# Two more seven-product pairs in a layer's first FFN, with their sums in the mixer and the ahead-splits gathered at one pair

## The chip, the cores and the metric

The kernel runs on one core of a Trainium2 chip. The metric is the device time of one execution in microseconds (us). Engines are named as in the profile: PE (matrix products; PEld is its loading of weights), DVE (vector), ACT (scalar), POOL (GpSimd) and SP, which here only issues DMA transfers. Each engine runs its instructions strictly in the order in which they were built; an instruction whose input, buffer or transfer is not ready holds up all behind it on its engine.

## The reference: what is computed

Two layers of a decoder trunk on 512 tokens plus 16 learned ones (528 columns), model width 1024. Each layer is a mixer (attention, two kinds of convolution, an output projection) and a gated FFN with 2816 hidden columns and a short causal convolution. The change touches the FFN of the first layer and what is prepared for it. Cut down:

```python
def ffn_sublayer(h, pre_g, post_g, w_up, conv_w, w_down):
    u = rms_norm(h, pre_g)
    z = jnp.einsum("bld,df->blf", u, w_up)
    z = causal_depthwise_conv(z, conv_w)
    g, up = jnp.split(z, 2, axis=-1)
    y = jnp.einsum("blf,fd->bld", jax.nn.silu(g) * up, w_down)
    return h + rms_norm(y, post_g)

for l in range(DEPTH):
    h = mixer_sublayer(h, ...)
    h = ffn_sublayer(h, ...)
```

## The kernel before

**Exact products in three passes.** Every float32 operand of a large product is split into a high part (a cast on ACT, `whi`, `shi`, `uhi`) and a low part (a subtraction on DVE, `wlo`, `slo`, `ulo`). A product is high by high, high by low, low by high. The 528 columns go in two halves of 264.

**The FFN.** The 2816 hidden columns are 22 blocks of 128. A *pair* f is block f of the gate and block f of the up-projection. Pairs run in three parts of 8, 7 and 7 (`PARTS`); after each part comes a stage *down*, eight output blocks m, whose results ACT copies (`yp`, L2410) or DVE adds. An ordinary pair is 2 blocks x 8 chunks of the width x 3 passes x 2 halves = 96 matmuls (L837).

**Seven products.** Some pairs are computed after Strassen's manner: the pair is a 2 x 2 block product, done as seven products of blocks (L2288) and not eight, 84 matmuls. For that the weights must be there as sums of blocks, which are made ahead into a DRAM tile `w_sum`, and taken from it as the blocks "c", "b" and "d". Weight block "b" is split into the tiles `shi` and `slo`, of which there is one buffer each; "c" goes to `whi`, `wlo` (three buffers). In a seven-product pair ACT copies the finished banks of PSUM to `zs` (L2373), which frees a bank for a later product of the same or the next pair.

**Who makes the sums.** `SUMS` has, for each layer, five places: ahead of time in the layer before; in the mixer; by *ticks* in the FFN (each pair, one step); in *down* of part 0; in *down* of part 1. In the mixer and by ticks a pair's sum is three copies from DRAM to DRAM, issued by SP (L545: two of 256 KB, one of 512 KB), and then three adding transfers issued by POOL (L534: 512 KB, 256 KB, 256 KB), each of which waits until the one before has landed. In *down* it is two loads by POOL into a spare tile, four additions on DVE and two stores by POOL (L589 to L601).

**The mixer's planner.** In the mixer a planner in the program (`Flow`) keeps a clock of its own for every engine and writes all engines' orders by costs and due times. The copies of the i-th pair in the mixer are due `SUM_EVERY * i` = 40 us of its clock apart, with priority 8; each transfer is planned at 0.9 us and 9 us until it has landed:

```python
for i, f in enumerate(sums_at(l, 1)):
    copies, *adds = sum_steps(l, f)
    tok = flow.op("sp", 2.0, copies, (Tok(flow.pe + SUM_EVERY * i),), prio=8, lat=SUM_LAT)
    for op in adds:
        tok = gp(SUM_US, op, tok, prio=8, lat=SUM_LAT)
```

On POOL the mixer also runs the causal masks of attention (L1651, tiles `p` and `pf`, exponentials that ACT makes at L1644). PE reads a masked tile in the product with the values (L1671).

**Ahead-splits.** While the FFN of layer 0 runs, six chunks of layer 1's input projection are loaded, split and stored to DRAM (`store_one`, L661 to L675): SP loads a chunk (L675), in a later call ACT casts it to `shi` (L666) and DVE subtracts to `slo` (L667), and POOL stores both (L670). They use the same single buffers `shi` and `slo` as block "b". `AHEAD_SPLITS` says at which pair f of the program the seven calls are written (f = 8 is the first pair of part 1); where their instructions stand on the engines is then set by the program's scheduler.

**h.** After part 0's pairs the tile `h` is copied to DRAM (L2384 and L2385, two transfers by SP) and is used as a spare buffer for weights from then on; it is loaded back after the last seven-product pair.

Of the kernel before, what the change touches and what calls it, by code (L numbers as in the profile page):

```python
# [18 lines left out]
KD = D // P  # L19
# [9 lines left out]
PARTS = (8, 7, 7)  # L29


SUMS = (((), (11, 12, 13), (15, 16), (17, 18), (19, 20)),
        ((8, 9), (10, 11, 12, 13), (15, 16), (17, 18), (19, 20)))
SEVEN = tuple(sorted(sum(places, ())) for places in SUMS)
NEXT_SUMS, AHEAD_SPLITS = 13, (8, 8, 9, 9, 10, 10, 11)
SUM_US, SUM_LAT, SUM_EVERY = 0.9, 9.0, 40.0
K2 = KD // 2
SB = K2 * P
# [351 lines left out]
def tile_hybrid_trunk(ctx: ExitStack, tc: tile.TileContext, xT, wflat, pv_d, out):  # L390
    nc = tc.nc
# [3 lines left out]
    def T(pool, shape, dt, tag, bufs=None):  # L395
        uid[0] += 1
        kw = {} if bufs is None else {"bufs": bufs}
        return pool.tile(list(shape), dt, tag=tag, name=f"{tag}_{uid[0]}", **kw)
# [92 lines left out]
    def load_h(pool, src, prio=0):  # L491

        t = T(pool, [P, KD, L], F32, "h", 1)
        at = {(hf, k0): flow.op("sp", dma_us(2 * H), lambda k0=k0, hf=hf: nc.sync.dma_start(
            t[:, k0:k0 + 2, half_sl(hf)], src[:, k0:k0 + 2, half_sl(hf)]), prio=prio + 3 * hf, lat=dma_lat(2 * H))
            for hf in range(2) for k0 in range(0, KD, 2)}
        return t, at

    dram = ctx.enter_context(tc.tile_pool(name="dram", bufs=1, space=bass.MemoryType.DRAM))
    h_dram = T(dram, [P, KD, L], F32, "h_dram")  # L500
# [48 lines left out]
    def sums_at(l, place):  # L549

        return SUMS[l][place] if l < DEPTH else ()

# [132 lines left out]
    def next_w():  # L685
        prefetch(1 + AHEAD)
        return ready.popleft()[1]
# [158 lines left out]
    def two(t):  # L846
        return t.rearrange("p (a b) -> p a b", a=2)
# [1181 lines left out]
    with tc.tile_pool(name="pre", bufs=2, reuse_waits="tile") as sp, tc.manual_schedule(engines=every):  # L2029
# [7 lines left out]
        h, h_at = load_h(sp, xT)  # L2037
# [56 lines left out]
    for l in range(DEPTH):  # L2094
# [23 lines left out]
        with tc.tile_pool(name=f"fp{l}", bufs=2, reuse_waits="tile") as fp:  # L2118
# [35 lines left out]
            with tc.manual_schedule(engines=every):  # L2154
                flow.yields = YF
                h, h_at = load_h(fp, xT if l == 0 else h_dram)
# [40 lines left out]
            seven = SEVEN[l]  # L2197
# [141 lines left out]
            def finish_pair():  # L2339
                if late_ups:  # L2340
                    late_ups.popleft()()
# [3 lines left out]
            for part, nf in enumerate(PARTS):  # L2345
                for f in range(f0, f0 + nf):
                    if g:
                        tick(g[max(g)][0][:, :1])
                    for _ in range(AHEAD_SPLITS.count(f) if l == 0 else 0):
                        store_one()  # L2350
                    if f in seven:
                        seven_pair(f)
                        if f == seven[-1]:
                            spare[0] = None
                            with tc.issue_after(last_load[0].ins):
                                for k in range(0, KD, 2):
                                    nc.sync.dma_start(h[:, k:k + 2], h_dram[:, k:k + 2])
                        continue
                    finish_pair()
                    if seven and f == 2:  # L2360
                        building[0] = normalised()
                    for i in (2 * f, 2 * f + 1):
                        if i < len(zs):
                            continue
                        if i < FIRST["w_out"]:
                            scaled(i, [first.ps[hf, i] for hf in range(2)])
                            continue
                        w = next_w()
                        ps = mmt((6, 2)[i % 2]) if ts else mmt()
                        mm3({hf: ps[:, hf, :iws[hf]] for hf in range(2)}, w, range(KD), u_in)  # L2370
                        if ts:
                            for (a, z), hf in zip(i_spans, range(2)):
                                nc.scalar.copy(zs[i % len(zs)][:, off + a - i0:off + z - i0], ps[:, hf, :z - a])  # L2373
                            continue
                        scaled(i, [ps[:, :, :H]] if i0 == 0 else [ps[:, hf, :iws[hf]] for hf in range(2)])
                    g[f] = ffn_gate(f)
                    if building[0] is not None and f < PARTS[0] - 1:
                        with tc.issue_after(mul_ins[0].ins):
                            build(5)
                finish_pair()  # L2380
                ks = list(range(nf))
                grhs = lambda b, k, hf, f0=f0: g[f0 + k][b][:, fw * hf:fw * (hf + 1)]
                if seven and part == 0:
                    for k in range(0, KD, 4):  # L2384
                        nc.sync.dma_start(h_dram[:, k:k + 4], h[:, k:k + 4])  # L2385
                    spare[0] = h
                if part < len(PARTS) - 1:
                    more = down_sums(l, part)
                    for op in more.pop(-1):
                        op()  # L2390
                    for some in ((0, 1), *((m,) for m in range(2, KD))):
                        ws = [next_w() for _ in some]
                        tiles = [mmt((4, 6, 2)[m % 3]) if seven else mmt() for m in some]
                        for group in (ks[:-1], ks[-1:]):
                            for w, ps in zip(ws, tiles):
                                where = {"start": group[0] == ks[0], "stop": group[-1] == ks[-1]}
                                if final:
                                    mm3({0: ps[:, 0, :2 * fw]}, w, group, lambda b, k, hf, f0=f0: g[f0 + k][b][:, :2 * fw], **where)
                                else:
                                    mm3({hf: ps[:, hf, :fw] for hf in range(2)}, w, group, grhs, **where)  # L2400
                        if building[0] is not None:
                            with tc.issue_after(glo_ins[0].ins):
                                build(99)
                        for m, ps in zip(some, tiles):
                            if final:
                                d, src = yp[:, m, t0:], ps[:, 0, :2 * fw]
                            else:
                                d, src = two(yp[:, m, t0:]), ps[:, :, :fw]
                            if part == 0:
                                evac = glo_ins[0] = nc.scalar.copy(d, src)  # L2410
                            else:
                                evac = nc.vector.tensor_add(d, d, src)
                            for op in more.pop(m, ()):
                                with tc.issue_after(evac.ins), tc.issue_after(last_low[0].ins):
                                    op()
                else:
                    assert not todo and not later and building[0] is None
                    if seven:
                        pools.pop().close()
                        pools.append(ExitStack())  # L2420
                        wx[0] = pools[1].enter_context(tc.tile_pool(name=f"wz{l}", bufs=WIDE, side="right", reuse_waits="tile"))
                    gpre = None if final else pvs[l + 1][1][:, _COLS["mix_pre_g"]:]
                    first = raw = rzs = None
                    if not final:
                        raw = list(zip(*[g[f0 + k] for k in range(nf)], y_pair(nf)))
                        raw = [[[t[:, half_sl(hf)] for t in ts] for ts in raw] if hf < 2 else None for hf in range(2)]
                        rzs = [rz[:, half_sl(hf)] if raw[hf] else None for hf in range(2)]
                        first = First(lambda b, k, hf, raw=raw: raw[hf][b][k] if raw[hf] else u_rhs(b, k, hf), [H, H], {})
                    with tc.issue_after(ghi_ins[NF - 2].ins), tc.manual_schedule(engines=every):
                        plan_begins()  # L2430
                        norms.factors([rs, zs[0][:, 2:]], h=APART)
                        flow.yields = YE
                        if not final:
                            plan_w(after_down, WE)
                        plan_w(len(chunks) if final else after_mixer[l + 1])
                        t_last = {nf - 2: [Tok(flow.now + 3.5)], nf - 1: [Tok(flow.now + 7.5)]}
                        finish(norms, h, {}, o_spans, ks, grhs, lambda k: t_last.get(k, []), yp,
                               gains("ffn_post_g"), gpre, SPLIT["ffn_w_down"], first, raw=raw, rzs=rzs, u_at=u_at)
                f0 += nf
# [51 lines left out]
```

## Time and profile before

| | us |
|---|---|
| profiled execution | 1262.1 |
| its span in the trace | 1260.4 |
| runs | 1263.05, 1264.51, 2452.8 |
| median of the three | 1264.51 |

One of the three runs took 2452.8 us, so that the median is the higher of the other two; the profiled execution lies within 0.2% of both. The page gives busy times of each engine, the chain of waits that ended last, groups of instructions by line, and the DMA issues with their median time to landing. The views of windows give busy time in chosen stretches, those of the timeline single instructions: start, duration, engine, line, operation, tiles, and in brackets the idle time before it on its engine with what ended it. Tiles' buffer numbers are left out.

### The profile page before, as it was taken

The page shows a single profiled execution, that of the slowest core. Times are in us where ns is not written, and L with a number is a line of the kernel's source. Part 1 is how long each engine was busy: PE and PEld are TensorE (multiplying, and loading weights), DVE is VectorE, ACT ScalarE, POOL GpSimd, SP SyncE. Part 2 cuts the span into 40 slices and gives each one's busy share as a digit, 9 for nine tenths or more (in the row PEclk, how much of TensorE's full clock was granted, in tenths as well). Part 3 has the DMA queues.
Part 4 walks back from the last instruction along what each step waited for, and adds up shares of the span by engine and source line. Part 5 has one row for each costly group of instructions (what it writes and reads, how often), then busy time and mean ns, then how long its engine had stood idle before and what let it go on. Part 6 is the DMA issues. An engine that isn't in the chain of part 4 may idle for free.

```text
span 1260.4 us, 24292 instructions
## 1 busy us (share of the span) xinstructions
PE 1244.2 (99%) x9554; PEld 1194.4 (95%) x9554; DVE 926.0 (73%) x1581; ACT 710.3 (56%) x1377; POOL 175.9 (14%) x360
## 2 busy tenths in 40 slices
PE   8999999999999999999999999999999999999997
PEld 8999898999999999999999988999999899989997
DVE  7887866589874776487688877756799748757954
ACT  7254576655444663476673545775554447526763
POOL 1323411001111001010003244110022000000000
PEclk9999999999999999999999999999999999999999
DMA  7267551726658755765652684547166565465611
GB/s 245 80 154 180 122 118 47 256 88 150 185 146 339 243 192 153 243 193 169 209 186 68 157 194 109 144 116 238 70 166 177 148 212 172 151 228 178 203 60 67
DMA packets 80755, 206.59 MB, mean 164 GB/s; under 512 B 8624, under 2 KB 18992, under 8 KB 80128
## 3 DMA queue, kind: packets, MB, share of 16 engines
q1 hardware_dynamic: 66976, 168.20, 42.1%
q0 software_dynamic: 13664, 36.84, 13.0%
q8 instruction: 75, 1.23, 0.4%
q14 instruction: 40, 0.33, 0.1%
HBM read 170.82 MB, written 50.60 MB: 176 GB/s over the span
## 4 chain that ended last, share of the span: by engine, by line
PE 94%; DVE 2%; ACT 1%; DMA 1%; POOL 1%; issue 0%; SPq 0%; DVEq 0%; ACTq 0%
PE psum L837 63%; PE psum L2288 17%; PE psum L1407 5%; PE psum L1671 3%; PE psum L1637 2%; PE psum L974 1%; PE psum L1593 1%; PE psum L1737 1%; PE psum L1323 1%; DMA raw<-in_w_dram 0%; POOL dm L1608 0%; DMA h<-in_x_dram 0%; DVE yp L1050 0%; DVE h L1060 0%; PE psum L1617 0%
## 5 line engine op out<-in xcount | busy, mean ns | idle before, releaser
L837 PE MATMUL psum<-y,whi 128*128 128x264 f32 (+3 forms) x1968 | 383.8, 299 | 0.8 <-DVE zs L989 0.7
L837 PEld LDWEIGHTS psum<-y,whi 128*128 128x128 f32 x1968 | 305.8, 188 | 13.7 <-DVE zs L989 0.9
L837 PE MATMUL psum<-uhi,whi 128*128 128x264 f32 (+1 forms) x1168 | 292.2, 289 | 1.5 <-ACT uhi L2069 0.8
L837 PE MATMUL psum<-ulo,whi 128*128 128x264 f32 (+1 forms) x1168 | 286.0, 284 | 0.6 <-DVE ulo L2071 0.4
L837 PE MATMUL psum<-uhi,wlo 128*128 128x264 f32 (+1 forms) x1168 | 285.3, 284 | 0.0
L837 PE MATMUL psum<-y,wlo 128*128 128x264 f32 (+3 forms) x984 | 274.0, 297 | 0.7 <-DVE wlo L793 0.7
L837 PEld LDWEIGHTS psum<-uhi,whi 128*128 128x128 f32 x1168 | 201.7, 189 | 5.9 <-issue 1.6
L837 PEld LDWEIGHTS psum<-ulo,whi 128*128 128x128 f32 x1168 | 201.8, 189 | 1.3 <-DVE ulo L2071 0.6
L837 PEld LDWEIGHTS psum<-uhi,wlo 128*128 128x128 f32 x1168 | 201.5, 189 | 0.0
L837 PEld LDWEIGHTS psum<-y,wlo 128*128 128x128 f32 x984 | 178.0, 188 | 6.4 <-DVE wlo L793 1.1
L2173 DVE SCALAR_TENSOR_TENSOR c<-zs,pv,c 128x528 f32<-128x528 f32 (+1 forms) x176 | 130.5, 756 | 21.2 <-ACT c L2171 19.9
L652 ACT CAST whi<-raw 128x1024 fp32r<-128x1024 f32 (+1 forms) x65 | 66.1, 1021 | 96.9 <-PE psum L837 74.3
L793 DVE TENSOR_TENSOR wlo<-raw,whi 128x1024 fp32r<-128x1024 f32 (+2 forms) x80 | 95.6, 1204 | 31.1 <-ACT whi L789 30.5
L789 ACT CAST whi<-raw 128x1024 fp32r<-128x1024 f32 (+2 forms) x80 | 81.7, 1030 | 26.3 <-PE psum L837 18.1
L653 DVE TENSOR_TENSOR wlo<-raw,whi 128x1024 fp32r<-128x1024 f32 (+1 forms) x65 | 76.9, 1183 | 20.9 <-ACT whi L652 20.9
L1153 DVE SCALAR_TENSOR_TENSOR cacc<-apad,pv,cacc 128x528 f32<-128x528 f32 x120 | 87.5, 771 | 0.1
L2288 PE MATMUL psum<-uhi,whi 128*128 128x258 f32 (+1 forms) x252 | 71.4, 284 | 0.0
L2288 PE MATMUL psum<-ulo,whi 128*128 128x258 f32 (+1 forms) x252 | 71.3, 283 | 0.0
L2288 PE MATMUL psum<-uhi,wlo 128*128 128x258 f32 (+1 forms) x252 | 70.8, 283 | 0.0
L2171 ACT ACTIVATE c<-zs,pv 128x528 f32<-128x528 f32 (+1 forms) x88 | 63.0, 727 | 6.8 <-DVE zs L2136 2.6
L2206 POOL COPY cols<-y 128x1 f32<-128x1 f32 x24 | 18.4, 767 | 334.7 <-ACT y L2187 334.4
L2288 PE MATMUL psum<-t,shi 128*128 128x258 f32 (+1 forms) x336 | 63.2, 283 | 0.0
(273 smaller groups left out, 2324.4 us busy)
## 6 DMA issues: line engine op xcount, KB each, us to landing
raw<-in_w_dram SPq DMA_DIRECT2D x114, 512.0 KB, 4.6
raw<-in_w_dram SPq DMA_DIRECT2D x30, 448.0 KB, 5.2
h<-in_w_dram SPq DMA_DIRECT2D x25, 512.0 KB, 4.7
raw<-w_sum SPq DMA_DIRECT2D x21, 512.0 KB, 5.2
h<-w_sum SPq DMA_DIRECT2D x21, 512.0 KB, 5.1
h<-in_w_dram POOLq DMA_DIRECT2D x16, 512.0 KB, 4.0
w_sum<-h POOLq DMA_DIRECT2D x16, 512.0 KB, 6.3
w_sum<-in_w_dram SPq DMA_DIRECT2D x26, 256.0 KB, 5.8
```

The source lines that it names most:

```text
L652: nc.scalar.copy(hi[:, :sz], raw[:, :sz])
L653: last_low[0] = nc.vector.tensor_sub(lo[:, :sz], raw[:, :sz], hi[:, :sz].bitcast(F32))
L789: nc.scalar.copy(box["hi"][:, :sz], box["raw"][:, :sz])
L793: nc.vector.tensor_sub(lo[:, :sz], box["raw"][:, :sz], box["hi"][:, :sz].bitcast(F32))
L837: nc.tensor.matmul(d, lhsT=w[a][:, k, cols], rhs=rhs(b, k, hf), start=start and i == 0 and p == 0, stop=stop and i == n - 1 and p == 2)
L1153: nc.vector.scalar_tensor_tensor(conv[j], in0=src, in1=conv[j], scalar=col("a_dw_w", CK * j + i), op0=ALU.mult, op1=ALU.add)
L1407: nc.tensor.matmul(ps[:n, :nw], lhsT=(uhi, ulo)[ui][:, k, P * b:P * b + n], rhs=w[wi][:, k % 4, :], start=k == 0 and p == 0, stop=k == KD ...
L1637: nc.tensor.matmul(s, lhsT=k[:, ka:ka + kn], rhs=q[:, s0:qz], start=i == 0, stop=i == 1)
L1671: nc.tensor.matmul(acc[:, s0 - qa:qz - qa], lhsT=vals[:, b].rearrange("p h d -> p (h d)")[:, o:o + P], rhs=box["p"], start=b == 0, stop=b ...
L2171: nc.scalar.activation(dst, src[:, 2:2 + 2 * fw], AF.Copy, scale=wtap(2, t))
L2173: nc.vector.scalar_tensor_tensor(dst, in0=src[:, i:i + 2 * fw], scalar=wtap(i, t), in1=dst, op0=ALU.mult, op1=ALU.add)
L2288: nc.tensor.matmul(psum[:, bank, :n7], lhsT=w[a][:, k0 + k, :], rhs=rhs(b, k), start=start and k == 0 and p == 0, stop=stop and k == K2 - ...
```

## The change

Three things. In layer 0, pairs 9 and 10 also become seven-product pairs, so that five pairs in place of three have their sums made in its mixer, and pair 17's sums move from *down* of part 0 to the ticks. The seven calls for ahead-splits are all written at f = 8. And `h` is copied to DRAM in two pieces at f = 2 and 3, not after the pairs of part 0.

```diff
-SUMS = (((), (11, 12, 13), (15, 16), (17, 18), (19, 20)),
+SUMS = (((), (9, 10, 11, 12, 13), (15, 16, 17), (18,), (19, 20)),
         ((8, 9), (10, 11, 12, 13), (15, 16), (17, 18), (19, 20)))
 SEVEN = tuple(sorted(sum(places, ())) for places in SUMS)
-NEXT_SUMS, AHEAD_SPLITS = 13, (8, 8, 9, 9, 10, 10, 11)
+NEXT_SUMS, AHEAD_SPLITS = 13, (8, 8, 8, 8, 8, 8, 8)
@@
                     if seven and f == 2:
                         building[0] = normalised()
+                    if seven and f in (2, 3):
+                        k = 4 * (f - 2)
+                        nc.sync.dma_start(h_dram[:, k:k + 4], h[:, k:k + 4])
@@
                 if seven and part == 0:
-                    for k in range(0, KD, 4):
-                        nc.sync.dma_start(h_dram[:, k:k + 4], h[:, k:k + 4])
                     spare[0] = h
```

Lines behind L2361 have numbers higher by three in the changed kernel, and by one behind L2385.

How instructions move is seen in the order in which each engine has them. First POOL at the end of mixer 0, before: `dm` are small operands, `p` and `pf` the masks of the last attention blocks.

```order
L1608 TENSOR_SCALAR dm_99_730<-ident_75,mcol_2440 128x128 x4
L1651 AFFINE_SELECT pf_2536<-pf_2536 128x128
L1651 AFFINE_SELECT pf_2550<-pf_2550 128x128
L1651 AFFINE_SELECT pf_2565<-pf_2565 128x128
L1651 AFFINE_SELECT p_79_687<-p_79_687 16x16
L1651 AFFINE_SELECT pf_2646<-pf_2646 128x128
L1651 AFFINE_SELECT pf_2682<-pf_2682 128x128
```

And now, where `w_sum_12` and `w_sum_13` are the sums of pairs 12 and 13:

```order
L1608 TENSOR_SCALAR dm_99_730<-ident_75,mcol_2445 128x128 x4
L534 DMA w_sum_12_106_738<-in_w_dram 128x2x512
L1651 AFFINE_SELECT pf_2542<-pf_2542 128x128
L1651 AFFINE_SELECT pf_2556<-pf_2556 128x128
L1651 AFFINE_SELECT pf_2571<-pf_2571 128x128
L1651 AFFINE_SELECT p_79_687<-p_79_687 16x16
L534 DMA w_sum_13_107_739<-in_w_dram 128x2x512
L534 DMA w_sum_13_107_739<-w_sum_13_107_739 128x512
L1651 AFFINE_SELECT pf_2652<-pf_2652 128x128
L534 DMA w_sum_12_106_738<-w_sum_12_106_738 128x512
L534 DMA w_sum_13_107_739<-w_sum_13_107_739 128x512
L1651 AFFINE_SELECT pf_2689<-pf_2689 128x128
```

The first two adds of pair 13 now stand ahead of the mask `pf_2652` (`pf_2646` before), and the third ahead of `pf_2689` (`pf_2682` before).

Second, SP at the same place, before: `raw` are weights, `h` the layer's input.

```order
L785 DMA raw_2335<-in_w_dram 128x1024
L785 DMA raw_2361<-in_w_dram 128x1024
L785 DMA raw_2557<-in_w_dram 128x1024
L785 DMA raw_2870<-in_w_dram 128x1024
L494 DMA h_2841<-in_x_dram 128x2x264 x7
```

And now:

```order
L785 DMA raw_2337<-in_w_dram 128x1024
L785 DMA raw_2363<-in_w_dram 128x1024
L545 DMA w_sum_12_106_738<-in_w_dram 128x512 x2
L545 DMA w_sum_12_106_738<-in_w_dram 128x1024
L785 DMA raw_2563<-in_w_dram 128x1024
L545 DMA w_sum_13_107_739<-in_w_dram 128x512 x2
L545 DMA w_sum_13_107_739<-in_w_dram 128x1024
L785 DMA raw_2881<-in_w_dram 128x1024
L494 DMA h_2852<-in_x_dram 128x2x264 x7
```

Pair 13's copies have come in behind the load `raw_2563` (`raw_2557` before).

Third, ACT from the end of the first *down* to f = 9, before: `yp` are results of *down*, L666 the ahead-splits' casts, `whi` weights.

```order
L666 CAST shi_4990<-raw_4865 128x1024
L2410 COPY yp_2833<-psum_67 128x528
L652 CAST whi_4802<-raw_4800 128x1024
L2410 COPY yp_2833<-psum_67 128x528
L666 CAST shi_4999<-raw_4997 128x1024
L652 CAST whi_4868<-h_2841 128x1024
L2410 COPY yp_2833<-psum_67 128x528
L666 CAST shi_5131<-h_2841 128x1024
L652 CAST whi_4923<-h_2841 128x1024
L2373 COPY zs_2834<-psum_67 128x264 x2
```

And now, with L2411 and L2376 for the lines L2410 and L2373, and `shi_5042` the block "b" of f = 9:

```order
L2411 COPY yp_2844<-psum_67 128x528
L666 CAST shi_4897<-raw_4895 128x1024
L652 CAST whi_4914<-raw_4912 128x1024
L2411 COPY yp_2844<-psum_67 128x528
L641 CAST y_517_5061<-raw_5059 128x512
L666 CAST shi_4905<-h_2852 128x1024
L641 CAST whi_4969<-h_2852 128x1024
L641 CAST shi_5042<-h_2852 128x1024
L2376 COPY zs_2845<-psum_67 128x264 x2
L652 CAST whi_5079<-h_2852 128x1024
L2376 COPY zs_2845<-psum_67 128x264 x2
```

Between the last two ahead casts and the copies `zs` there now stands the cast `shi_5042`; all three casts write the one buffer `shi`. The first two of the ahead-splits' casts have moved to f = 5 and 6.

## The prediction

> **What bounds the kernel.** The page first, its totals and its chain of waits:
>
> ```profile
> span 1260.4 us, 24292 instructions
> PE 1244.2 (99%) x9554; PEld 1194.4 (95%) x9554; DVE 926.0 (73%) x1581; ACT 710.3 (56%) x1377; POOL 175.9 (14%) x360
> PE 94%; DVE 2%; ACT 1%; DMA 1%; POOL 1%; issue 0%; SPq 0%; DVEq 0%; ACTq 0%
> ```
>
> PE is busy 1244.2 of 1260.4 us and carries 94% of the chain. So two things alone can move the time: the number of matmuls, and any moment at which PE has to wait. POOL's 14% looks harmless, but the question for POOL is not how much it works but whether it stands still in front of something that PE needs.
>
> Next the windows (PE alone) around the two pairs that change their form, 9 and 10, and around the first seven-product pair of layer 0, which is f = 11 now:
>
> ```profile
> core 0: us, PE busy (x), PEclk, DMA share, GB/s
> 411.11:434.52 23.41, 23.41 (x195) 1.00 0.77 268
> 434.52:457.71 23.19, 22.84 (x188) 1.00 0.63 199
> 1.26:6.38 5.12, 5.12 (x23) 1.00 0.85 272
> 6.38:8.97 2.59, 2.59 (x23) 1.00 1.06 397
> ```
>
> The first stretch is f = 9 and 10, dense; the second starts with f = 11 and loses 0.35 us (23.19 long, 22.84 busy). The last two rows are the start of the kernel: the same 23 matmuls take 5.12 us, then 2.59, so PE runs at half rate after standing idle. (The PEclk column shows 1.00 for both, so rates are counted here from matmuls.)
>
> **1. The saving.** A seven-product pair issues 84 matmuls in place of 96. Two pairs make 24 fewer, at 23.41 / 195 = 0.120 us each: **−2.9 us**. That holds only while DVE and ACT keep up. For that, the windows of all engines:
>
> ```profile
> core 0: us, PE busy (x) PEld busy (x) DVE busy (x) ACT busy (x) POOL busy (x), PEclk, DMA share, GB/s
> 322.00:357.00 35.00, 35.00 (x289) 35.00 (x288) 31.66 (x46) 17.05 (x23) 5.03 (x8) 1.00 0.55 151
> 1025.74:1072.59 46.85, 46.85 (x393) 46.85 (x391) 35.39 (x46) 33.16 (x60) 0.53 (x1) 1.00 0.55 168
> ```
>
> The second row is layer 1, where six seven-product pairs already stand in a row: PE full, DVE at 35.39 and ACT at 33.16 of 46.85. So five in a row cost nothing beyond the saving. The first row is the stretch of pairs f = 5 and 6, into which the first two of the seven ahead-splits come in the new order (a cast of about 1.05 on ACT and a subtraction of about 1.2 on DVE each). DVE has 3.34 us left there, against 2.4 wanted; I take 0, bounds 0 and 1.2.
>
> **2. Copying h to DRAM.** In the built order the two copies stand on SP between the same two weight loads as before: 0. So does pair 17, whose sums leave the down stage for ticks on POOL at f = 9 to 12: its loads, four additions on DVE and stores go, three copies and three adding transfers come, with nobody near: 0.
>
> **3. Five pairs' sums in mixer 0: a new wait on POOL.** For each pair, SP issues three copies and POOL three adding transfers, each waiting for the landing of the one before. POOL works in order. Today the third and last pair there is done with before the mixer's end; now pair 13's adds stand between two masks of the attention's last blocks (the order of POOL is shown ahead). What the transfers and masks take, from the page's DMA rows, the two lines' landings (L545 the copies, L534 the adds) and the timeline:
>
> ```profile
> w_sum<-in_w_dram SPq DMA_DIRECT2D x26, 256.0 KB, 5.8
> w_sum<-in_w_dram POOLq DMA_DIRECT2D x13, 512.0 KB, 7.7
> w_sum<-w_sum POOLq DMA_DIRECT2D x26, 256.0 KB, 5.0
> DMA to landing us min/median/max: 4.8/5.9/7.9
> DMA to landing us min/median/max: 4.6/5.5/9.3
> 58.34 1.24 POOL L534 DMA_DIRECT2D w_sum<-in_w_dram  x1 [0.39 <-issue]
> 66.22 0.89 POOL L534 DMA_DIRECT2D w_sum<-w_sum  x1 [6.63 <-DMA w_sum<-in_w_dram]
> 195.09 0.33 SPq L785 DMA_DIRECT2D raw<-in_w_dram  x1
> 203.60 1.30 POOL L1651 TENSOR_SCALAR_AFFINE_SELECT pf<-pf 128x128 f32<-128x128 f32 x1 [5.62 <-ACT pf L1644]
> 206.68 0.29 POOL L1651 TENSOR_SCALAR_AFFINE_SELECT pf<-pf 128x128 f32<-128x128 f32 x1 [1.78 <-ACT pf L1644]
> 205.11 0.38 PE L1671 MATMUL psum<-pf,vals 128*128 128x128 f32 x2
> 208.25 0.83 PE L1671 MATMUL psum<-pf,vals 128*128 128x400 f32 x2
> ```
>
> Pair 13's copies stand on SP behind the weight load at 195.09, which waits for its buffer. Three issues of about 0.6 put the second copy at 196.1, landed at 196.1 + 5.8 = 201.9. There POOL has long been waiting. The first add goes at 202.0; the second, by the rows 58.34 and 66.22, 7.9 later, at 209.9; it takes 0.9, and then comes the mask of 203.60, done at 211.1. The PE product that reads it stands at 205.11, 0.2 after its mask, so it now starts at 211.3: 6.2 late. The third add waits for the second's landing, 209.9 + 5.0 + 0.3 = 215.2; with 0.85 for the issue and 0.3 for the mask, the product that stands at 208.25 starts at 216.6: 8.4 late, and this includes the first 6.2. Between the two lie 3.1 us of PE work; at half rate after the first wait they would end at 217.6, 1.0 past 216.6, and I take 0.4 of it. **+8.8 us.** Bounds: with copies at 4.8 and adds at 4.6 both times, the second mask's product stands at about 211.8, +3.5; with 7.9 and 9.3 at about 224, +16. PE has no other work in its order to put in between.
>
> A page of the Trainium skill speaks against this term: "DMA: Bandwidth & Descriptors", section "Anatomy of one DMA — SWDGE (gpsimd) path", fits 2.0 us plus bytes over 436e3 for each transfer, thus about 3.2 us for 512 KB and 2.6 for 256 KB. By that, as an estimate, pair 13's adds are through by 206.9 and the masks in time: the term would be 0. The rows above, at 7.7 and 5.0, don't agree.
>
> **4. All ahead-splits at f = 8: a new wait on ACT.** The split of the "b" weights of a seven-product pair writes the same single buffer, shi, as the ahead-splits, and each cast there must wait until POOL has stored the contents before. In the new ACT order two ahead casts stand straight ahead of f = 9's own cast of shi, and behind that the copy zs that frees PE's next bank. The timeline of before, the stores' rows and L670's landings:
>
> ```profile
> w_split<-shi POOLq DMA_DIRECT2D x6, 512.0 KB, 6.2
> DMA to landing us min/median/max: 3.0/6.4/8.4
> 397.37 1.05 ACT L666 CAST shi<-raw 128x1024 fp32r<-128x1024 f32 x1 [2.52 <-issue]
> 402.50 1.05 ACT L666 CAST shi<-h 128x1024 fp32r<-128x1024 f32 x1 [1.83 <-DVE wlo L653]
> 410.37 1.06 ACT L666 CAST shi<-raw 128x1024 fp32r<-128x1024 f32 x1
> 412.90 0.66 ACT L2373 COPY zs<-psum 128x264 f32<-128x264 f32 x2
> 436.49 0.51 PE L2288 MATMUL psum<-t,whi 128*128 128x264 f32 x2 [0.35 <-ACT zs L2373]
> ```
>
> The two steps between these casts are 5.13 and 7.87 us. With the stores' median of 6.2, the cast's 1.05 and some 0.35 for the issue, one step is 7.6, which I take. The cast at 397.37 is the first of the three in the new order as well, so the others go at 405.0 and 412.6. Behind the last: cast to 413.6, the copies zs of one half to 414.3, a weight cast to 415.3, the copies of the other to 415.9. PE wants that bank, as the row 436.49 shows for f = 11, 436.49 − 0.35 − 434.52 = 1.62 after the pair's start: 411.11 + 1.62 = 412.7. A wait of 3.2, and f = 11's 0.35 goes: **+2.9 us**. Bounds: at 5.13 a step the cast is done at 408.7 and the term 0; at 8.4 a store a step is 9.8 and the term 7.8.
>
> **Sum.** 1262.1 (the profiled execution, span 1260.4) − 2.9 + 8.8 + 2.9 = 1270.9. The two runs of the same kind, 1263.05 and 1264.51, average with it to 1263.2, 1.1 above, so I set the time at **1272.0 us**, 0.7% over the mean before. Two per cent, 25 us, is about what a measurement here can tell from no change.
>
> **Rivals.**
> - *Only the mixer's wait.* f = 9's wait is hidden because the stores land early, as the 5.13 step shows they can: 1272.0 − 2.9 = 1269.1. Chance 0.25.
> - *Only f = 9's wait.* Pair 13's copies get out of SP ahead of where I put them, because the load of 195.09 gets its buffer earlier. From about 8 us earlier on, nothing is late there: 1272.0 − 8.8 = 1263.2. For it: SP only waits there. Against: that load's buffer is freed by work whose order doesn't change. 0.06.
> - *Neither:* transfers land quickly in both places: 1263.2 − 2.9 = 1260.3. The skill's fit, named above, leads here. Against: the medians of 5.0 to 7.7. 0.08.
> - *Half rate after both waits,* each by up to 5.12 − 2.59 = 2.5 us, of which 0.4 is in the sum: up to 1272 + 4.6, in the middle 1275. 0.06.
> - *Slower by over 2%.* PE falls to half rate in a wait and stays there. The first rows show 5.12 / 23 = 0.223 us a matmul against 0.113, so each microsecond at half rate loses about half. The 17 us from 1272 to 1288.5 need 34 us at half rate on end. Nothing after 6.38 us shows such a stretch. 0.02.
>
> The Trainium skill's "TensorE: Matmul & The Clock Gate", section "Part 1: The HAM clock gate (the "warmup" mystery)", has the clock halved after an idle window of about 3.4 us until about 3.4 us of busy time have passed. By that, as an estimate, each wait costs up to 1.7 us more, and the sum 1274; the two rows at the start agree with it, no later row shows a wait long enough.
>
> **Chances.** Forecast (both waits) 0.52; mixer only 0.25; f = 9 only 0.06; neither 0.08; half rate after both 0.06; persistent half rate 0.02; something that I don't see, faster by over 2%, 0.01. The bounds of the likeliest are 1262.1 + 1.1 − 2.9 + (3.5 to 16) + (0 to 7.8) = 1264 to 1284, both ends of everything at once being rare. I give 1260 to 1280: it takes in the two cases with one wait and half of "neither". All but the last two cases lie within 25 us of before: faster 0.01, same 0.97, slower 0.02.
>
> **What would show it.** Right: PE idle for 5 to 7 us ahead of L1671 near 205, put down to POOL's mask L1651, and again for 1 to 3 us a few microseconds later; in POOL's rows an L534 issue directly ahead of each. At f = 9 a wait of about 3 us ahead of L2288, put down to ACT zs, with an L666 or L641 cast of shi before it that waits for a store. f = 9 to 13 take 84 matmuls each at 0.12 us. Wrong: no idle PE near 205 (then pair 13's adds got through earlier, or the masks come first); a step of shi near 5 us; PE waiting in f = 5 or 6 for DVE.

## The result and the profile after

| | before | changed |
|---|---|---|
| median of the runs, us | 1263.78 | 1280.91 |
| profiled execution, us | 1262.1 | 1281.63 |
| its span, us | 1260.4 | 1279.9 |

The changed kernel is slower by a ratio of 1.0135 (95% interval 1.0115 to 1.0155), 17.1 us between the medians; the forecast was 1272.0, at most 1280. A further run of the kernel before, 1262.97, makes its median 1263.78. Of the changed kernel's four runs (1278.67 to 1281.63) the profiled one is the slowest, and the kernel before has its fastest time, 1262.1, in the profiled execution, so the traces show 19.5 us of difference, 2.4 more than the medians.

The page of the changed kernel, its totals and its chain by engine:

```profile
span 1279.9 us, 24305 instructions
PE 1246.2 (97%) x9530; PEld 1194.2 (93%) x9530; DVE 928.0 (73%) x1585; ACT 715.2 (56%) x1385; POOL 185.0 (14%) x369
PE 88%; DMA 4%; DVE 4%; issue 2%; ACT 2%; POOL 1%; SPq 0%; DVEq 0%; ACTq 0%; POOLq 0%
```

PE issues 24 matmuls fewer (9530 for 9554), as it should, and yet is busy 2.0 us longer, and 6% of the chain have gone from PE to transfers and other engines. Where, a table by stage shows. Both kernels were cut at the same instructions of PE: the start, the mixer's last stretch with attention, the output projection behind it, the FFN's first pairs, f = 9, and f = 15 with all that follows. The columns are the window, its length and PE's busy time with its instructions, the granted clock, the DMA share and GB/s. First the kernel before, then the changed one.

```profile
0.00:168.49 168.49, 164.08 (x1224) 1.00 0.59 154
168.49:213.91 45.42, 45.04 (x331) 1.00 0.27 77
213.91:276.15 62.24, 62.24 (x501) 1.00 0.52 180
276.15:411.11 134.96, 134.96 (x1109) 1.00 0.62 192
411.11:518.13 107.02, 106.67 (x879) 1.00 0.67 212
518.13:1260.40 742.27, 731.17 (x5521) 1.00 0.54 158
```

```profile
0.00:170.53 170.53, 163.97 (x1223) 1.00 0.58 152
170.53:226.69 56.16, 47.58 (x332) 0.91 0.59 137
226.69:288.95 62.26, 62.26 (x502) 1.00 0.52 180
288.95:426.72 137.77, 135.64 (x1107) 1.00 0.64 199
426.72:536.81 110.09, 105.59 (x856) 0.98 0.69 207
536.81:1279.90 743.09, 731.14 (x5521) 1.00 0.54 158
```

The end of the mixer takes 10.7 us more, of which 8.2 are idle and 2.5 are the same matmuls at a lower granted clock (0.91 in the mean). The stage that holds pairs 9 and 10 takes 3.1 more, though it has fewer matmuls. The two stages with 2.0 and 2.8 more, at the start and from the first pairs to f = 8, were not forecast; e9 and e5 below show that both come and go between executions of one order of instructions.

**The mixer's end.** PE's timeline, then POOL's, of the changed kernel, and the window from the wait's end to the next masked product:

```profile
207.06 0.28 PE L837 MATMUL psum<-y,wlo 128*128 128x264 f32 x1
215.54 0.79 PE L1671 MATMUL psum<-pf,vals 128*128 128x128 f32 x2 [8.20 <-POOL pf L1651]
221.04 0.83 PE L1671 MATMUL psum<-pf,vals 128*128 128x400 f32 x2
```

```profile
197.55 1.87 SPq L545 DMA_DIRECT2D w_sum<-in_w_dram  x3
205.69 1.16 POOL L534 DMA_DIRECT2D w_sum<-in_w_dram  x1 [5.64 <-DMA w_sum<-in_w_dram]
214.33 0.85 POOL L534 DMA_DIRECT2D w_sum<-w_sum  x1 [7.48 <-DMA w_sum<-in_w_dram]
214.90 0.58 POOL L1651 TENSOR_SCALAR_AFFINE_SELECT pf<-pf 128x128 f32<-128x128 f32 x1
219.40 0.81 POOL L534 DMA_DIRECT2D w_sum<-w_sum  x1 [3.10 <-DMA w_sum<-w_sum]
219.94 0.57 POOL L1651 TENSOR_SCALAR_AFFINE_SELECT pf<-pf 128x128 f32<-128x128 f32 x1
```

```profile
215.54:221.04 5.50, 5.50 (x19) 0.56 0.69 97
```

This is the wait as it was foreseen: POOL does nothing but wait for landings, twice, 5.6 and 7.5 us, and only then comes the mask that PE needs. The work between the two masked products then takes 5.50 us at a granted clock of 0.56, where it took 3.14 before. The third add came out as a second cause at the same place: its mask is done at 220.5, so that PE could not have gone on much before 220.7 even at full rate. The lower clock and the third add thus lie on top of each other: either alone would have cost most of the 2.5 us behind the first wait. The Trainium skill's page "TensorE: Matmul & The Clock Gate", section "Part 1: The HAM clock gate (the "warmup" mystery)", has the array at half clock after an idle window of about 3.4 us, until some 3.4 us of work; after 8.2 us of idling this trace agrees, but as a limit for a single wait the figure doesn't hold in these runs (the last section), and there the measurement decides.

**f = 9.** PE, ACT, DVE and POOL of the changed kernel, in this order, and the window of PE between its two waits:

```profile
432.08 0.81 PE L2288 MATMUL psum<-t,whi 128*128 128x264 f32 x2 [3.63 <-ACT zs L2376]
436.39 0.39 PE L2288 MATMUL psum<-uhi,wlo 128*128 128x264 f32 x1 [0.87 <-DVE wlo L653]
416.15 1.05 ACT L666 CAST shi<-raw 128x1024 fp32r<-128x1024 f32 x1 [6.13 <-issue]
420.43 1.05 ACT L666 CAST shi<-h 128x1024 fp32r<-128x1024 f32 x1 [0.86 <-DMA w_split<-shi]
429.19 1.04 ACT L641 CAST shi<-h 128x1024 fp32r<-128x1024 f32 x1 [3.53 <-DMA w_split<-shi]
431.63 0.67 ACT L2376 COPY zs<-psum 128x264 f32<-128x264 f32 x2
426.11 1.23 DVE L667 TENSOR_TENSOR slo<-h,shi 128x1024 fp32r<-128x1024 f32 x1 [4.74 <-ACT whi L641]
433.98 1.23 DVE L642 TENSOR_TENSOR slo<-h,shi 128x1024 fp32r<-128x1024 f32 x1 [5.50 <-DMA w_split<-slo]
435.12 1.22 DVE L653 TENSOR_TENSOR wlo<-h,whi 128x1024 fp32r<-128x1024 f32 x1
427.63 0.53 POOL L670 DMA_DIRECT2D w_split<-slo  x1 [5.33 <-DVE slo L667]
```

```profile
432.08:435.52 3.44, 3.44 (x14) 0.51 0.62 251
```

The first wait, 3.63 us, is the one that was forecast: three casts of `shi` in a chain of stores, and the copy `zs` behind the last. The second, 0.87, is its twin on the other engine, which the forecast did not follow: `slo` also has one buffer, its chain of stores runs 4.8 us later (the subtraction at 433.98 against the cast at 429.19), and behind it on DVE stands the low part `wlo` of a weight that PE wants. Between the two waits PE ran at a granted clock of 0.51, which cost it some 1.7 us (half of 3.44). That time was not lost on top: `wlo` was done at 436.35 because `slo` had waited for its store until 433.98, so at full rate PE would have stood that much longer before the same moment. DVE's chain is the one that ended last here.

### The profile page after: what moved, and what is told of

The parts are those of the page before. It is cut to its first block, busy times and chain, and to the rows that moved or that the text cites. A ratio compares the mean times of both kernels' runs of the same rounds, so it can differ in the third digit from the quotient of the medians.

```text
span 1279.9 us, 24305 instructions
## 1 busy us (share of the span) xinstructions
PE 1246.2 (97%) x9530; PEld 1194.2 (93%) x9530; DVE 928.0 (73%) x1585; ACT 715.2 (56%) x1385; POOL 185.0 (14%) x369
## 4 chain that ended last, share of the span: by engine, by line
PE 88%; DMA 4%; DVE 4%; issue 2%; ACT 2%; POOL 1%; SPq 0%; DVEq 0%; ACTq 0%; POOLq 0%
PE psum L837 56%; PE psum L2288 18%; PE psum L1407 4%; PE psum L1671 3%; PE psum L1637 2%; PE psum L974 1%; DMA w_sum<-in_w_dram 1%; PE psum L1593 1%; DMA raw<-in_w_dram 1%; DMA h<-in_w_dram 1%; PE psum L1737 1%; PE psum L1323 1%; DMA w_split<-shi 1%; POOL dm L1608 0%; DMA h<-in_x_dram 0%
## 5 line engine op out<-in xcount | busy, mean ns | idle before, releaser
L837 PE MATMUL psum<-uhi,whi 128*128 128x264 f32 (+1 forms) x1104 | 278.3, 289 | 1.9 <-ACT uhi L2069 0.8
L837 PE MATMUL psum<-ulo,whi 128*128 128x264 f32 (+1 forms) x1104 | 272.3, 284 | 0.6 <-DVE ulo L2071 0.4
L837 PE MATMUL psum<-uhi,wlo 128*128 128x264 f32 (+1 forms) x1104 | 271.2, 283 | 0.0
L837 PEld LDWEIGHTS psum<-uhi,whi 128*128 128x128 f32 x1104 | 191.3, 188 | 6.5 <-issue 1.6
L837 PEld LDWEIGHTS psum<-ulo,whi 128*128 128x128 f32 x1104 | 191.5, 188 | 1.4 <-DVE ulo L2071 0.6
L837 PEld LDWEIGHTS psum<-uhi,wlo 128*128 128x128 f32 x1104 | 191.0, 188 | 0.0
L2288 PE MATMUL psum<-uhi,whi 128*128 128x258 f32 (+1 forms) x276 | 78.3, 284 | 0.0
L2288 PE MATMUL psum<-uhi,wlo 128*128 128x258 f32 (+1 forms) x276 | 77.3, 283 | 0.9 <-DVE wlo L653 0.9
L2288 PE MATMUL psum<-ulo,whi 128*128 128x258 f32 (+1 forms) x276 | 78.1, 284 | 0.0
L2288 PE MATMUL psum<-t,shi 128*128 128x258 f32 (+1 forms) x368 | 69.3, 283 | 0.0
```

The source lines that it names most:

```text
L837: nc.tensor.matmul(d, lhsT=w[a][:, k, cols], rhs=rhs(b, k, hf), start=start and i == 0 and p == 0, stop=stop and i == n - 1 and p == 2)
L2288: nc.tensor.matmul(psum[:, bank, :n7], lhsT=w[a][:, k0 + k, :], rhs=rhs(b, k), start=start and k == 0 and p == 0, stop=stop and k == K2 - ...
```

## The experiments

Each ratio is against runs of the kernel before on the same chip.

**e1: the five pairs closer together.** In layer 0 the copies are due 25 us apart:

```diff
-(Tok(flow.pe + SUM_EVERY * i),)
+(Tok(flow.pe + (25.0 if l == 0 else SUM_EVERY) * i),)
```

> The changed kernel, with the copies of mixer 0's pairs due 25 us apart and not 40 (layer 1 unchanged); all five pairs' transfers are kept, and pair 13's adds now stand ahead of the last block of attention. Theory (POOL stands before the masks, then PE runs at half rate): the 8.2 us of idle PE ahead of L1671 near 207 and the half rate behind it go, 10.7 us less, about 1270. Rival (the two additional pairs' transfers slow what else runs, wherever they stand): within 3 us of the changed kernel, about 1280.

1277.18 us, ratio 1.0104 (1.0086 to 1.0122). The end of the mixer was back at 45.45 us, but PE's waits (us in total, times, longest) show new ones earlier:

```profile
PE psum L1593 <- DMA k<-pair_hi: 3.7, 1, 3.7
PE psum L1593 <- DMA k<-sq: 1.7, 1, 1.7
```

Pair 10's and pair 11's copies, issued near 74 and 104 us, now fell in with the small transfers of `k` near 76 and 109 us, for which PE waits: 3.7 us at the second, 3.6 in e4 with the same spacing, at most 2.3 there in any run with 40 us. Neither theory alone is right: the place in POOL's order costs, and so does the place among other transfers.

**e5: only pair 13 later.** Its due time goes from 160 to 180 us, and all three of its adds stand behind the masks that they held up:

```diff
-(Tok(flow.pe + SUM_EVERY * i),)
+(Tok(flow.pe + (180.0 if (l, i) == (0, 4) else SUM_EVERY * i)),)
```

> The changed kernel, with pair 13's sums in mixer 0 due at 180 us of the planner's clock and not 160, so that its adds stand on POOL behind the last mask; the other four pairs stay where they are, and all transfers are kept. Theory (it is POOL's place, not the transfers as such): the 8.2 us wait before L1671 and the half rate behind it go, 10 to 11 us less, about 1270, and no new wait as with 25 us spacing, since the transfers come where no small q and k transfers run. Rival (five pairs' transfers cost 4 to 6 us wherever they stand, as the waits for k near 80 and 112 with 25 us spacing suggest): about 1275.

1272.08 us (1268.38 to 1275.93), ratio 1.0070 (1.0044 to 1.0096), 8.8 us less than the changed kernel (8.3 when each is taken against the kernel before on its own chip). Windows of PE, the mixer's end, the output projection behind it, and the stage from f = 9:

```profile
169.51:214.94 45.43, 45.05 (x332) 1.00 0.50 124
214.94:277.94 63.00, 62.51 (x502) 1.00 0.68 212
277.94:412.90 134.96, 134.96 (x1107) 1.00 0.65 203
412.90:524.33 111.43, 106.40 (x855) 0.97 0.69 204
```

The end of the mixer is at 45.43, that of the kernel before, with all five pairs' transfers kept. The loss in this stage was the place of one pair's three adds on POOL. Where they are now they cost 0.8 us at most (63.00 for 62.24).

**e2: the ahead-splits ahead of the first down.**

```diff
-NEXT_SUMS, AHEAD_SPLITS = 13, (8, 8, 8, 8, 8, 8, 8)
+NEXT_SUMS, AHEAD_SPLITS = 13, (5, 5, 6, 6, 7, 7, 7)
```

> The changed kernel, with the calls for ahead-splits at f = 5, 5, 6, 6, 7, 7, 7, so that all their casts stand ahead of the first down stage. Theory (the chain of casts and stores through the one buffer shi, and slo behind it, delays f = 9): PE's wait of 3.6 us near 428 and that of 0.9 for DVE's wlo go, some 5.5 to 6 us less, about 1275; the wait near 400 stays. Rival (f = 9 waits for its own weights, whose loads come late): the wait stays, about 1280. Rival for the wait near 400 (the ahead-splits' loads stand before the weights' on SP): it goes here, another 2.2 us.

1280.29 us, ratio 1.0129 (1.0113 to 1.0145): no gain. Its windows from the first pairs and from f = 9, and PE's waits there:

```profile
287.49:430.80 143.31, 139.12 (x1107) 0.98 0.66 199
430.80:534.75 103.95, 103.85 (x855) 1.00 0.69 207
PE psum L837 <- DVE wlo L653: 2.2, 2, 1.7
PE psum L837 <- ACT whi L652: 2.0, 2, 1.4
```

f = 9's wait is gone, as the theory has it: the stage takes 103.95 us for 110.09. The six casts of the ahead-splits, now between 322 and 369 us, make waits near 353 and 370 instead, and that stage takes 143.31 for 134.96 in e5. What was taken from one pair was given to others.

**e3: pair 17 back in down.** `SUMS` for layer 0 with `(15, 16), (17, 18)` in place of `(15, 16, 17), (18,)`:

> The changed kernel, with pair 17's sums back in the down stage of part 0. Theory (with one pair fewer in down, the spare tile is given back earlier, and the first weight load into it waits for the store of the sums): PE's 1.3 + 0.5 us of waiting near 400 go, about 2 us less; the ahead-splits' order moves as well, so that f = 9's wait may change by some us either way; 1275 to 1280. Rival (the loads of the ahead-splits are what holds the weights): the wait near 400 stays, about 1281.

1288.35 us, ratio 1.0191 (1.0175 to 1.0208), outside what either theory gave. No wait near 400; but with pair 17 in down, none of the ahead-splits' casts stands in f = 5 and 6 any more and one has moved past the start of f = 9, where the seven-product pairs' own casts use `shi`. PE waited six times from 423 to 473, five of them for 1.3 to 2.8 us. As a test of pair 17's place it failed, since it moved the splits too.

**e4: the three edits of e1, e2 and e3 together.**

> All three edits together: spacing 25, ahead-splits at f = 5 to 7, pair 17 in down; pairs 9 and 10 stay seven-product pairs. Theory: all losses go and the 24 matmuls saved remain, 2.9 us under the kernel before, about 1261. Rival (five pairs in the mixer cost something wherever they stand, or the seven-product form saves nothing in place): at the kernel before or above, 1264 or more.

1278.23 us, ratio 1.0108 (1.0088 to 1.0129). A wait as in e1 for `k` (3.6) and waits as in e2 in the pairs (up to 3.3 and 3.4) were both there: the theory's sum failed because two of its edits only moved their waits.

**e7: no ahead-splits at all**, and pair 13 late. `MASK`, which picks the chunks, is all zeros; layer 1 then splits these chunks itself.

> Pair 13 late, and no ahead-splits at all: the six chunks of layer 1's input projection are loaded and split in layer 1's mixer like the others. Pair 17 stays with the ticks. Theory: from the first pair to the last of layer 0, f = 9's wait goes (5.9 us); the wait near 400 stays, since it comes from the sums' store in the spare tile; what layer 1 loses for it is unknown, 0 to 8 us; 1264 to 1273. Rival for the wait near 400 (the splits' loads ahead of the weights on SP): it goes too.

1265.92 us, ratio 1.0023 (1.0009 to 1.0038). The windows from the start, from the first pairs, from f = 9 and from f = 15:

```profile
0.00:173.20 173.20, 166.07 (x1223) 0.99 0.57 150
280.91:415.74 134.83, 134.83 (x1107) 1.00 0.49 141
415.74:519.57 103.83, 103.83 (x856) 1.00 0.69 205
519.57:1268.30 748.73, 733.63 (x5521) 1.00 0.52 153
```

PE is dense from the first pairs to f = 14. The second last row is what the seven-product form saves: 107.02 − 103.83 = 3.2 us, of which 0.35 is the wait that f = 11 had. Layer 1 pays for the missing splits: from f = 15 to the end 748.73 us for 742.27. The wait near 400 was gone as well; but e5, which has the changed kernel's order in these pairs on every engine, has none either (134.96, dense). So neither pair 17's leaving down nor the order makes it by itself. What differs is when one load landed: in the trace of the changed kernel ACT's cast at 400.71 had waited 5.41 us for its weights, in e5 the same cast, at 387.10, 1.05 us.

**e6, e8, e12: one ahead-split for each pair.** All three have pair 13 late. e6 and e8 call the ahead-splits at f = 3, 4, 5, 6, 7, 8, 8, e6 with pair 17 in down, e8 with the ticks; e12 is e6 with the calls at f = 4, 5, 6, 7, 8, 8, 8.

> As before (pair 13 late), and besides the ahead-splits called at f = 3, 4, 5, 6, 7, 8, 8, one for each pair, with pair 17 back in down. Theory (one cast, store and load in 11.7 us of a pair fit, two didn't): no wait at f = 9, none near 400, small ones in f = 4 to 8; 24 matmuls saved remain, 1261 to 1264. Rival (the splits cost some 5 us in the pairs wherever they stand, as with the calls at 5 to 7): about 1266.

> Pair 13 late, ahead-splits called at f = 3, 4, 5, 6, 7, 8, 8, and pair 17 left with the ticks as in the changed kernel. Beside the run with pair 17 in down this shows what pair 17's place is worth when the splits are out of the way. Theory: the wait near 400 is there and costs 2 us; about 1264. Rival: no wait near 400, and no difference to the other.

> Pair 13 late, pair 17 in down, six chunks with the calls at f = 4, 5, 6, 7, 8, 8, 8: one split fewer in the early pairs and one more in down than in the run with calls from f = 3. Theory (a split in a pair costs some half microsecond where DVE is nearly full, one in down nothing): 1262, 0 to 1 us less than there. Rival (in down it comes close to f = 9's cast of shi): 1 to 3 us more.

| | us | ratio (95%) | first pairs to f = 8, us | from f = 9, us |
|---|---|---|---|---|
| e6 | 1262.94 | 1.0000 (0.9990 to 1.0009) | 136.77 | 103.84 |
| e8 | 1267.59 | 1.0044 (1.0029 to 1.0060) | 141.60 | 103.92 |
| e12 | 1260.85 | 0.9979 (0.9971 to 0.9988) | 134.81 | 103.59 |

All three have the whole saving from f = 9 on. They differ in what the splits cost in the early pairs: in e6 1.4 us of waits for DVE's `zs`, in e8 1.2 for these and 1.8 for ACT, with PE at a granted clock of 0.50 from 360.57 to 363.98 behind it, in e12 nothing. For e8 neither the theory's wait near 400 nor the rival's equal time came. What pair 17's place does isn't shown by itself, since the splits move with it. e12 in the same windows, from the start, from the first pairs and from f = 9:

```profile
0.00:172.53 172.53, 165.73 (x1224) 0.99 0.58 150
280.22:415.03 134.81, 134.81 (x1107) 1.00 0.69 219
415.03:518.62 103.59, 103.59 (x856) 1.00 0.64 197
```

e12 beats both kernels: 2.8 us under the one before in medians, and 20 under the changed one.

**e9: the moves alone.** The changed kernel with the `SUMS` of the kernel before:

> The kernel before, with the copies of h at f = 2 and 3 and all seven calls for ahead-splits at f = 8, but its own thirteen... that is, its own pairs and places of sums (9 and 10 ordinary, three pairs in the mixer). Theory (the moves by themselves cost nothing: on ACT the casts of shi stand in the same order as before, and f = 9 and 10 don't use shi): the time before, 1263 to 1264. Rival (the gathered splits are what costs in f = 8 and 9): up to 6 us more.

1262.62 us, ratio 0.9994 (0.9986 to 1.0003): the copies of h and the gathered calls cost nothing as long as f = 9 and 10 don't use `shi`. Its window from the start shows something else:

```profile
0.00:172.64 172.64, 165.18 (x1224) 0.99 0.58 150
```

With the instructions of the kernel before in this stretch it took 172.64 us and not 168.49; in e7 and e12 it took 173.20 and 172.53, in e5 and e6 169.5 and 169.3. It scatters by 4 us from one execution to the next, and since the changed kernel has this same order there too, the 2.0 us in its trace need not be the change's.

**e10 and e11: fewer splits.** As e6, but only four chunks split ahead, called at f = 4, 5, 6, 7, 8 and at 6, 7, 8, 8, 8.

> Pair 13 late, pair 17 in down, and only four chunks of layer 1 split ahead, called at f = 4, 5, 6, 7, 8; two chunks more are split in layer 1's mixer. Theory (in the run with six spread splits 2 us were left as waits in the pairs, which need fewer splits to go): 1.5 us less in layer 0's pairs than there, 0 to 2 us more in layer 1; 1261 to 1264. Rival (layer 1 pays a microsecond for each chunk, as six chunks cost 6 us there): 1264 or more.

> As the one before, with the calls at f = 6, 7, 8, 8, 8, so that two of the four casts stand in the first down stage: 1261 to 1264 by the same theory, and without the wait near 324 for DVE, which came with the first split in f = 4.

1263.20 us, ratio 0.9996 (0.9987 to 1.0005), and 1262.06 us, ratio 0.9985 (0.9977 to 0.9994). Neither waits in layer 0's pairs; both wait 1.8 us for DVE at the start of layer 1 (e12: 0.7). In the medians e12 is 1.2 us under e11, but their intervals overlap, so whether six splits are better than four isn't decided.

## Why the prediction was wrong, point by point

The forecast named both mechanisms that made the change slower, with their places; it fell short in size, by 8.9 us between 1272.0 and 1280.91. By the stages of the traces 1.9 of these are the mixer's end (10.7 for 8.8) and 3.1 the stage from f = 9, where the saving and the wait were to cancel; 0.6 is the median of the kernel before, 1263.78 for 1263.2. The last 3.3 us belong to neither term.

- **Term 1, the saving, −2.9:** right. Free of waits the stage from f = 9 takes 103.6 to 103.9 us, and e12 shows the gain in whole runs, 2.8 us.
- **Term 2, h and pair 17, 0:** right for h and for the gathered calls by themselves (e9). Pair 17's place wasn't free of consequences as "with nobody near" put it: it moves the ahead-splits in the built order (e3 against the changed kernel).
- **Term 3, the mixer, +8.8:** right in place and mechanism, shown by e5; it measured 10.7. The part that was mis-sized is the first wait, 8.2 us and not 6.2. This stage starts 2.0 us later, and the copies went out where the forecast had them (197.55 for 195.5 + 2.0). But the copy that the first add needs took 7.0 us to land where 5.8 was taken, the add was issued 0.6 behind the landing and not 0.1, at 205.69, and the second add followed 8.6 us behind and not 7.9. What comes after the first wait was sized well: 2.2 for the third add and 0.4 for the clock, 2.6, measured 2.5. The range's upper bound for this term, +16, held it.
- **Term 4, f = 9, +2.9:** the step that failed is the assumption that ACT's chain is the only one there. DVE's chain through `slo` ended later, and it set when PE went on: the stage takes 110.09 us, 6.2 to 6.5 more than where it is free of waits, in place of the 3.2 of the forecast. That the wait for `zs` itself came out near its size, 3.63 us, is in part luck. Against the pair's start ACT's first of the three casts went 3.2 us later than forecast (416.15 with the pair at 426.72, against 397.37 with 411.11), and the two steps to the third took 4.28 and 8.76 us, 13.0 together and not 15.2. (The term's upper bound, 7.8, comes out at 7.6 when it is added up again.)
- **The clock.** "Half rate after both waits" was a rival with a chance of 0.06 and a middle of 1275. PE did run at half rate at both places, 2.5 and about 1.7 us of time lost to it, but that explains little of the miss. At each place another chain ended at nearly the same time, the third add's mask at 220.5 for PE's 221.04, and DVE's `wlo` at 436.35 for 436.39; at full rate PE would have waited there instead (an estimate from these times; no run has one without the other).
- **The rest.** The trace's waits near 400 and 110 us, 4.9 us in two stages, vary between executions: e5 has the changed kernel's order in the pairs and no wait there, e9 the order before and the longer start. How much of them is in the medians is open, but some of it seems to be the change's. e5's median is 8.8 us above the kernel before, and its trace, of the fastest of its four runs, accounts for 5.2 (111.43 for 107.02 from f = 9, and 0.8), so that 3.6 are left there too, close to the 3.3 of the changed kernel. In e6 and e12, with the splits elsewhere, only about one is left. What makes these microseconds isn't shown.
- **The rivals.** "Only the mixer's wait", "only f = 9's" and "neither" fall: both waits are there. The Trainium skill's fit from "DMA: Bandwidth & Descriptors", section "Anatomy of one DMA — SWDGE (gpsimd) path", by which "neither" would have come, gives 3.2 us for a 512 KB transfer; here 8.6 us lie between the issue of one, at 205.69, and that of the next, at 214.33, which waits for it. The measurement decides.

## What to carry to other kernels

A wait for a transfer that stands in an engine's order costs whatever stands behind it, so ask of every added transfer on POOL which instruction comes next there, and move the due time of that one item: 20 us of planned time took away 10.7 us in this stage of the trace here, with all transfers kept. Where a single buffer is filled by one engine and read by a store, follow both halves of the pair through their engines, and count the steps against the time between uses: six casts that are 8.7 us or more apart were free in e12, while six that are as close as 4.7 moved the wait in e2 and did not remove it. And where two chains end at one place, price the one that ends last: PE's slow stretch at f = 9, in front of the later wait, added nothing of its own.

## What the runs showed of the hardware that was not expected

After idling of 3.6 us PE ran at half rate as it does at the start of the kernel: matmuls behind it come 0.22 us apart. But the length of one wait doesn't decide it here. In e12 half rate followed a wait of 1.9 us near 110, in e4 full rate followed one of 3.35 us. These windows of PE are the work behind e12's wait, then e4's wait and the work behind it:

```profile
111.64:115.40 3.76, 3.76 (x19) 0.55 0.43 118
374.92:378.27 3.35, 0.00 (x1) 1.00 1.04 383
378.27:382.00 3.73, 3.73 (x30) 1.00 0.61 216
```

A stretch of the mixer with one and the same order of instructions took 168.5 to 173.2 us from one execution to another, a part of it (up to 2.3 us) in a wait ahead of L1593, the product of `k` and `q`, whose operands come by small transfers; in kernels this tight a single trace can show 4 us that the change has not made.
